# A two-layer decoder trunk: the residual stream held in DRAM by chunks and added to by accumulating transfers, and nine more pairs of weight columns with a second Strassen unit

## The chip, the cores and the metric

The kernel runs on one core of one Trainium2 chip. Its engines are TensorE (PE: matmuls and transposes), VectorE (DVE), ScalarE (ACT), GpSimd (POOL) and SyncE (SP, which only issues transfers); 16 DMA engines move data between DRAM and SBUF, the on-chip memory of 128 partitions. TensorE's sums lie in PSUM. The metric is the device time of one execution in microseconds.

## The reference

The input x is 256 rows of 2048 values, all float32. Each of two layers does

```python
h = rms_norm(x, mix_norm[l])
proj = h @ w_in[l]                                  # 2048 x 7680: q, k, v, uv, gate logits
branch_a = sliding_window_attention(q, k, v, sinks[l]) @ w_attn_branch[l]
branch_b = chunked_sgu(jax.nn.gelu(uv), w_spatial[l], ...) @ w_sgu_branch[l]
gates = jax.nn.sigmoid(gate_logits)
merged = gates[..., :D_MODEL] * branch_a + gates[..., D_MODEL:] * branch_b
x = x + merged @ w_out[l]                           # first residual
h2 = rms_norm(x, ffn_norm[l])
x = x + (jax.nn.silu(h2 @ w_gate[l]) * (h2 @ w_up[l])) @ w_down[l]   # second residual
```

The inner width of the last line (w_gate, w_up, w_down) is 5632. Nearly all the work is products of 256 rows of activations with these weights.

## The kernel before, in words

**Tiles.** The 256 rows are two tiles of 128 (NT = 2). Weights are taken by columns of 512 (a chunk, CW) and by 256 rows of the inner dimension, so that a weight tile is 128 partitions x 1024 values, 512 KB. Activations are kept transposed, in units of 512 inner rows, that is two weight tiles deep.

**Precision.** Each float32 operand is split in two parts that TensorE takes: a high half (ScalarE's copy, `whi` for weights, `uh` for activations) and a low half (VectorE's subtraction, `wlo`, `ul`). A product is three matmuls of 512 columns: high by high, high by low, low by high (L353, L354). One weight tile against both row tiles is 12 matmuls.

**Strassen units.** Columns are often taken in pairs, two chunks against the same activations (gate and up columns of w_gate and w_up; two chunks of w_down, w_out and others). A pair's first unit (number `WINO` = 0) is computed by Strassen's scheme in Winograd's form: the 2 x 2 blocks are the two row tiles, the two inner halves of the unit and the two chunks. Seven products P1 to P7 of 6 matmuls stand for eight. For it VectorE makes four differences of weight tiles (L242, `raw<-raw,raw`), in place; and, once for each unit of activations, four sums (`sums`, L512) from a plain copy of the unit (`flat`), split into `sh` and `sl`. P3, P6 and P7 use these. With `two` a pair does so for unit 1 as well. In the row of gate/up pairs that is done where r > 0 and the pair is one of the round's first three (L190).

**Order.** `plans` lists all pairs and single chunks; `entries` are their weight tiles in TensorE's order, where the P entries of a pair (its head) are woven into the last entries of the plan ahead. `step` works off one entry; `stream.next` keeps the loads 7 entries ahead (`W_LOAD`), the splits 4 (`W_SPLIT`) and the differences 6 (`W_SUM`). `tick` counts slots of two products (some 12 matmuls), and `after(n, fn)` puts work n slots later: turning an activation, its parts, squares for a norm. TensorE runs in the order as written; the other engines' orders are made by a scheduler that models the time, and are fixed in the program. SP issues all weight loads. GpSimd issues the small gathers that finish a transposition (`tt<-box`, 16 transfers of 32 KB behind VectorE's 32 x 32 block transposes), or SP and GpSimd halve them.

**Buffers.** The loaded weight tiles lie in five buffers (`wraw`) plus one buffer for each of the four tiles of a first Strassen unit; those of a second unit take a slot of the pool `big` (26 slots of 4 KB per partition), which also holds activations, boxes, hidden chunks and sums. Split halves have four buffers each (`wsp`). `tmp` has five of 2 KB. The residual stream, `xs`, is one constant tile of 16 KB per partition.

**The stages of a layer**: the input projection (`in`), attention's and the spatial unit's branches (`att`, `sgu`), the output projection (`mix`, two pairs of w_out), then three rounds over the 11 chunks of the inner width, of 4, 4 and 3. A round is so many gate/up pairs (`hidden`), then two w_down pairs over what they made (`hid`). `residual` (L942) adds a product's two row tiles to `xs` straight from PSUM on VectorE (L950); behind the output projection, and behind the last round of layer 0, it also turns the new x for the next norm (`Norm.unit`) and squares it; at the end it stores.

**A unit turned twice.** `again=True` turns a unit of x a second time, on GpSimd's queue, only to make the plain copy and the sums of it for Strassen: for unit 0 of the input projection of layer 0 (L597), and for unit 1 of each layer's gate/up pairs (L963, 24 slots behind the output projection). `summed` (L524) makes them instead from the unit's own halves, `flat = uh + ul`.

**The start.** SP loads x in four chunks with the first weights between; a short transposition gives the norm's columns (`first_cols`), ScalarE scales the transposed x by them (`uh<-pt,first_cols`, L452), and splits the first weights (L257).

## Time and profile before

| | |
|---|---|
| median of 3 runs | 2427.58 us (2427.35 to 2428.07) |
| the profiled execution | 2427.18 us |
| its span, first to last instruction | 2425.5 us |
| bytes read from and written to HBM | 475.27 MB, 2.10 MB |
| instructions | 31042 |

Times in the profile are microseconds, unless ns is written. PE, PEld (loading the stationary operand, beside the matmuls), DVE, ACT and POOL stand with busy time, share and number of instructions. In the groups of instructions a row has line, engine, operation, out<-in with shapes, count, busy time and mean ns of one, then the engine's idle time ahead of them and what ended it; "(+1 forms)" means that another shape is counted in. Line numbers are those of the kernel before, which the change moves down by 4 to 28. In rows by time the first two numbers are start and duration, and a bracket holds idle time and its releaser. In windows each engine has its busy time with the number of instructions, then PEclk, the clock granted to TensorE (1.00 is full), the mean busy share of the DMA engines, and GB/s.

### The profile page before, as it was taken

The numbers are of one execution on the slowest core, as the hardware profiler recorded it, in microseconds if no ns is written. First come the engines' busy times: TensorE is split into PE (matmuls) and PEld (weight loads), VectorE is DVE, ScalarE is ACT, GpSimd is POOL, SyncE is SP. The second block draws the span as 40 slices with busy tenths as digits, with TensorE's granted clock in tenths as the row PEclk, the third lists the DMA queues.
The fourth block names the chain that finished last, engine by engine and source line by source line (L and its number), as shares of the span: only waits on it lengthen the run. The fifth ranks groups of instructions, "written<-read, shape, count | busy, mean of one in ns | idle before, by whom it ended". The sixth has DMA issues, their size and how long they took to land.

```text
span 2425.5 us, 31042 instructions
## 1 busy us (share of the span) xinstructions
PE 2417.2 (100%) x10768; PEld 1984.1 (82%) x10768; DVE 2025.9 (84%) x2346; ACT 1492.1 (62%) x1878; POOL 290.7 (12%) x545
## 2 busy tenths in 40 slices
PE   9999999999999999999999999999999999999999
PEld 7877888888888888888888778888888888888887
DVE  6789787897978997899887897878878789978996
ACT  5577555566655675567655775555666556655664
POOL 3100001032110011001101000011322101110010
PEclk9999999999999999999999999999999999999999
DMA  9665678576767657766747557775767676667664
GB/s 294 213 187 162 182 201 251 175 252 208 225 209 235 208 175 227 237 200 178 231 149 261 173 158 195 217 227 181 249 207 235 204 245 185 204 211 236 210 181 146
DMA packets 278989, 504.62 MB, mean 208 GB/s; under 512 B 27760, under 2 KB 39120, under 8 KB 278832
## 3 DMA queue, kind: packets, MB, share of 16 engines
q1 hardware_dynamic: 262288, 485.83, 64.4%
q0 software_dynamic: 16224, 16.54, 2.6%
q8 instruction: 84, 1.38, 0.2%
q14 instruction: 73, 0.60, 0.1%
q10 hardware_dynamic: 320, 0.27, 0.0%
HBM read 475.27 MB, written 2.10 MB: 197 GB/s over the span
## 4 chain that ended last, share of the span: by engine, by line
PE 96%; DMA 2%; DVE 1%; issue 0%; ACT 0%; POOL 0%; SPq 0%; DVEq 0%; ACTq 0%
PE acc L353 63%; PE acc L354 31%; DMA raw<-in_w_in_dram 2%; PE psc L798 1%; PE po L850 0%; DVE wlo L258 0%; PE psg L933 0%; PE ppt L835 0%; ACT whi L257 0%; PE pt L466 0%; POOL rq L325 0%; DVE ul L457 0%; SPq L290 0%; DVE xs L950 0%; DVE box L423 0%
## 5 line engine op out<-in xcount | busy, mean ns | idle before, releaser
L257 ACT ACTIVATE whi<-raw 128x1024 fp32r<-128x1024 f32 (+1 forms) x1086 | 1142.5, 1058 | 843.1 <-PE acc L354 559.9
L258 DVE TENSOR_TENSOR wlo<-raw,whi 128x1024 fp32r<-128x1024 f32 (+1 forms) x1087 | 1314.9, 1219 | 344.5 <-ACT whi L257 329.1
L353 PE MATMUL acc<-whi,uh 128*128 128x512 f32 x2954 | 1154.5, 391 | 0.9 <-ACT uh L452 0.9
L353 PE MATMUL acc<-wlo,uh 128*128 128x512 f32 x2954 | 1150.7, 390 | 2.0 <-DVE wlo L258 2.0
L354 PE MATMUL acc<-whi,ul 128*128 128x512 f32 x2954 | 1150.0, 389 | 0.0
L353 PEld LDWEIGHTS acc<-whi,uh 128*128 128x128 f32 x2954 | 554.5, 188 | 121.3 <-issue 3.8
L353 PEld LDWEIGHTS acc<-wlo,uh 128*128 128x128 f32 x2954 | 554.6, 188 | 119.3 <-DVE wlo L258 4.5
L354 PEld LDWEIGHTS acc<-whi,ul 128*128 128x128 f32 x2954 | 554.6, 188 | 115.8 <-DVE ul L457 0.5
L429 POOL DMA_DIRECT2D tt<-box x496 | 243.0, 497 | 1632.2 <-DVE box L423 747.5
L242 DVE TENSOR_TENSOR raw<-raw,raw 128x1024 f32<-128x1024 f32 x252 | 307.4, 1220 | 1.7 <-DMA raw<-in_w_up_dram 0.8
L353 PE MATMUL acc<-whi,sh 128*128 128x512 f32 x504 | 197.9, 393 | 0.0
L353 PE MATMUL acc<-wlo,sh 128*128 128x512 f32 x504 | 196.5, 390 | 0.0
L354 PE MATMUL acc<-whi,sl 128*128 128x512 f32 x504 | 196.2, 389 | 0.0
L353 PEld LDWEIGHTS acc<-whi,sh 128*128 128x128 f32 x504 | 94.6, 188 | 22.1 <-issue 2.3
L353 PEld LDWEIGHTS acc<-wlo,sh 128*128 128x128 f32 x504 | 94.7, 188 | 19.9 <-DVE wlo L258 0.8
L354 PEld LDWEIGHTS acc<-whi,sl 128*128 128x128 f32 x504 | 94.6, 188 | 19.8
L379 DVE TENSOR_TENSOR kept<-acc,kept 128x512 f32<-128x512 f32 x102 | 69.8, 684 | 10.3 <-PE acc L354 10.3
L382 ACT ACTIVATE acc<-kept 128x512 f32<-128x512 f32 x102 | 59.6, 587 | 5.1 <-DVE kept L379 4.2
L950 DVE SCALAR_TENSOR_TENSOR xs<-acc,xs 128x512 f32<-128x512 f32 (+1 forms) x66 | 42.0, 668 | 8.4 <-PE acc L354 8.0
L325 POOL TENSOR_TENSOR rv<-ve,neg_half 128x4 f32<-128x4 f32 x8 | 10.2, 1272 | 260.7 <-DVE ve L898 241.8
L376 ACT ACTIVATE kept<-acc 128x512 f32<-128x512 f32 x51 | 30.3, 594 | 8.4 <-PE acc L354 7.9
L820 ACT ACTIVATE pr<-pr,negm 128x128 f32<-128x128 f32 x64 | 24.9, 389 | 14.1 <-DVE negm L811 14.1
(145 smaller groups left out, 840.9 us busy)
## 6 DMA issues: line engine op xcount, KB each, us to landing
raw<-in_w_in_dram SPq DMA_DIRECT2D x239, 512.0 KB, 4.8
raw<-in_w_gate_dram SPq DMA_DIRECT2D x176, 512.0 KB, 4.6
raw<-in_w_up_dram SPq DMA_DIRECT2D x176, 512.0 KB, 5.0
raw<-in_w_down_dram SPq DMA_DIRECT2D x176, 512.0 KB, 5.0
raw<-in_w_out_dram SPq DMA_DIRECT2D x64, 512.0 KB, 6.2
raw<-in_w_attn_branch_dram SPq DMA_DIRECT2D x64, 256.0 KB, 6.3
raw<-in_w_sgu_branch_dram SPq DMA_DIRECT2D x32, 512.0 KB, 5.9
tt<-box POOLq DMA_DIRECT2D x496, 32.0 KB, 4.4
```

The lines of the kernel that those rows point to most:

```text
L242: self.last = nc.vector.tensor_tensor(out=self.raws[d], in0=self.raws[x], in1=self.raws[y], op=ALU.subtract)
L257: self.high = nc.scalar.activation(hi[:, i, :], raw[:, i, :], AF.Copy)
L258: self.last = nc.vector.tensor_tensor(out=lo[:, i, :], in0=raw[:, i, :], in1=hi[:, i, :].bitcast(F32), op=ALU.subtract)
L353: nc.tensor.matmul(ps, a, part[:, kk, :], start=first and kk + n == 0, stop=False, skip_group_check=True)
L354: nc.tensor.matmul(ps, b, hi[:, kk, :], start=False, stop=kk == 1, skip_group_check=True)
L376: nc.scalar.activation(p.kept[:, 1, :], a[0], AF.Copy)
L379: nc.vector.tensor_tensor(out=p.kept[:, int(tag == "P7"), :], in0=a[1], in1=p.kept[:, 1, :], op=ALU.add)
L382: nc.scalar.activation(ps, p.kept[:, t, :], AF.Copy)
L429: q.dma_start(dst[j * B:(j + 1) * B, i], box[i * B:(i + 1) * B, j])
L798: nc.tensor.matmul(pscore[:, i, :nk], self.qT[pair // 4][j * HD:(j + 1) * HD, pair % 4, t * P:(t + 1) * P], self.kT[j * HD:(j + 1) * HD, : ...
L820: self.exps = nc.scalar.activation(pr4[:, h, :], pr4[:, h, :], AF.Exp, bias=nm_[:, h:h + 1], accum_out=den[:, h:h + 1])
L950: nc.vector.scalar_tensor_tensor(out=xs[:, t, sl], in0=sums[t][:, i * w:(i + 1) * w], scalar=scale, in1=xs[:, t, sl], op0=ALU.mult, op1=AL ...
```

## The change

**The residual stream.** `xs` goes. At the start x is loaded into four slots of `big`, one per chunk, which serve the first norm alone. The stream's home is a DRAM buffer of four chunks, `held_x` (512 KB each). Behind the output projection and behind layer 0's last round, the four chunks are fetched into slots (issued by GpSimd, slots 2 to 5 of that residual's first pair; for layer 0's output projection from the input x itself), added to on VectorE as before, and stored to `held_x` five slots later. Behind rounds 0 and 1 the chunks are not fetched: ScalarE copies the two row tiles out of PSUM (`part`), and GpSimd issues one transfer a chunk that adds it to `held_x`. The last residual fetches, adds, and stores the output. In all 16 accumulating transfers, 12 stores and 16 fetches (four of them from x).

**Buffers.** 16 KB of `xs`, one buffer of `tmp` and three small constants make room for 31 slots of `big` instead of 26; `tmp` has 4.

**More second Strassen units.** `FFN_TWO` names the gate/up pairs (round, place) that have two: all of round 1's four, the last of round 0, and the three of round 2, in both layers: (0, 3) and (1, 3) are new, four pairs. `HID_TWO` names five w_down pairs (layer, round, first chunk): both of round 0 in each layer, and the second of round 1 in layer 1. Nine pairs in all.

**Sums from the halves.** The three second turnings (`again`) are replaced by `summed`, and the hidden unit 1 of the rounds with a `HID_TWO` pair gets its sums the same way, 16 slots (or 9) behind the pair that made it.

```diff
 W_SPLIT = 4
-W_TWO = 24
+X_FETCH = 2
+HID_TWO = (1, 2, 2), (0, 0, 0), (1, 0, 0), (0, 0, 2), (1, 0, 2)
+W_HID = 16
+FFN_TWO = (1, 0), (1, 1), (1, 2), (2, 0), (2, 1), (2, 2), (0, 3), (1, 3)
+W_TWO = 20
 W_SUM = 6
...
-    big = ctx.enter_context(tc.tile_pool(name="big", bufs=26))
+    big = ctx.enter_context(tc.tile_pool(name="big", bufs=31))
     wraw = ctx.enter_context(tc.tile_pool(name="wraw", bufs=5))
     wsp = ctx.enter_context(tc.tile_pool(name="wsp", bufs=4))
-    tmp = ctx.enter_context(tc.tile_pool(name="tmp", bufs=5))
+    tmp = ctx.enter_context(tc.tile_pool(name="tmp", bufs=4))
...
         for r, (f0, f1) in enumerate(ROUNDS):
             for f in range(f0, f1):
                 plans.append(pair(("ffn", l), w_gate[l, :, f * CW:(f + 1) * CW], w_up[l, :, f * CW:(f + 1) * CW], f == 0,
-                                  two=r > 0 and f - f0 < 3))
+                                  two=(r, f - f0) in FFN_TWO))
             c_ = cols_of(w_down[l, f0 * CW:f1 * CW, :], NCH)
-            plans += [pair(("hid", l, r), c_[j], c_[j + 1], j == 0) for j in range(0, NCH, 2)]
+            plans += [pair(("hid", l, r), c_[j], c_[j + 1], j == 0, two=(l, r, j) in HID_TWO) for j in range(0, NCH, 2)]
...
-    xs = const.tile([P, NT, D], F32, name="xs")
+    def x_rows(dram, c):
+        return dram[0, :, c * CW:(c + 1) * CW].rearrange("(t p) n -> p t n", p=P)
+
+    kept_x = ctx.enter_context(tc.tile_pool(name="kept_x", bufs=1, space=bass.MemoryType.DRAM))
+    held_x = [kept_x.tile([P, NT, CW], F32, tag=f"x{c}", name=f"held_x{c}") for c in range(NCH)]
+    xs = [slot([P, NT, CW], name="x") for _ in range(NCH)]
     for c in range(NCH):
         for t in range(NT):
-            nc.sync.dma_start(xs[:, t, c * CW:(c + 1) * CW],
-                              x[0, t * P:(t + 1) * P, c * CW:(c + 1) * CW])
+            nc.sync.dma_start(xs[c][:, t, :], x[0, t * P:(t + 1) * P, c * CW:(c + 1) * CW])
         stream.load(LOAD_BY[c])
...
         def __init__(self, cols, soon=False):
             self.cols, self.soon = cols, soon
-            self.units = [None] * NCH
+            self.units, self.x = [None] * NCH, [None] * NCH
         def squares(self, c):
             for t in range(NT):
                 junk = temp(name="junk")
-                nc.scalar.activation(junk, xs[:, t, c * CW:(c + 1) * CW], AF.Square,
+                nc.scalar.activation(junk, self.x[c][:, t, :], AF.Square,
                                      accum_out=self.ss[t][:, c:c + 1])
         def unit(self, c, on_pe=False, again=False, queue=nc.gpsimd, late=0):
-            transposed(self.units, c, xs[:, :, c * CW:(c + 1) * CW], cols=self.cols[:, 4 * c:4 * c + 4],
+            transposed(self.units, c, self.x[c], cols=self.cols[:, 4 * c:4 * c + 4],
                        on_pe=on_pe, again=again, queue=queue, late=late,
                        wino=WINO_FIRST if again else None if c != WINO or on_pe else WINO_IN if self.soon else WINO_NORM)
...
     for c in range(NCH):
         after(3 + c, lambda c=c: squared(c))
     after(7, lambda: norm.finish())
-    after(10, lambda: norm.unit(WINO, again=True))
+    after(10, lambda: summed(norm.units, WINO, (1, 2, 4)))
...
                 nc.vector.scalar_tensor_tensor(out=u, in0=pg[:, i], scalar=vcols[:, bc:bc + 1], in1=u,
                                                op0=ALU.add, op1=ALU.mult)
-    def residual(key, nxt=None, scale=1.0, store=False):
+    def residual(key, nxt=None, scale=1.0, store=False, first=False):
+
+        xt = {}
+
+        def fetched(j):
+            xt[j] = slot([P, NT, CW], name="x")
+            nc.gpsimd.dma_start(xt[j], x_rows(x, j) if first else held_x[j])
         def chunk(j, sums):
+            if j not in xt:
+                part = slot([P, NT, CW], name="part")
+                for t in range(NT):
+                    nc.scalar.activation(part[:, t, :], sums[t], AF.Copy)
+                nc.gpsimd.dma_start(held_x[j], part, accum_op=ALU.add)
+                return
             for t in range(NT):
                 n = 2 if store and j == NCH - 1 else 1
                 w = CW // n
                 for i in range(n):
-                    sl = slice(j * CW + i * w, j * CW + (i + 1) * w)
-                    nc.vector.scalar_tensor_tensor(out=xs[:, t, sl], in0=sums[t][:, i * w:(i + 1) * w], scalar=scale,
-                                                   in1=xs[:, t, sl], op0=ALU.mult, op1=ALU.add)
+                    sl = slice(i * w, (i + 1) * w)
+                    nc.vector.scalar_tensor_tensor(out=xt[j][:, t, sl], in0=sums[t][:, sl], scalar=scale,
+                                                   in1=xt[j][:, t, sl], op0=ALU.mult, op1=ALU.add)
                     if store:
                         eng = nc.sync if i == 0 else nc.scalar
-                        eng.dma_start(out[0, t * P:(t + 1) * P, sl], xs[:, t, sl])
+                        eng.dma_start(out[0, t * P:(t + 1) * P, j * CW + i * w:j * CW + (i + 1) * w], xt[j][:, t, sl])
             if nxt is not None:
+                nxt.x[j] = xt[j]
+                after(5, lambda: nc.gpsimd.dma_start(held_x[j], xt[j]))
                 last = j == NCH - 1 and not nxt.soon
                 after(1 if last else 2, lambda: nxt.unit(j, j > 0 and nxt.soon, queue=None if last or j == WINO and not nxt.soon else nc.gpsimd,
                                                          late=-2 if last else 0))
...
                 if j == NCH - 1:
                     after(4, lambda: nxt.finish())
                     if not nxt.soon:
-                        after(W_TWO, lambda: nxt.unit(WINO + 1, again=True))
+                        after(W_TWO, lambda: summed(nxt.units, WINO + 1, (1, 2, 4)))
         for j in range(0, NCH, 2):
+            if j == 0 and (nxt is not None or store):
+                for i in range(NCH):
+                    after(X_FETCH + i, lambda i=i: fetched(i))
             product_pair(key, lambda sums: chunk(j, sums), lambda sums: chunk(j + 1, sums))
         return nxt
...
             merged(j, product(("sgu", l)))
             tick()
-        norm = residual(("mix", l), nxt, scale=0.5)
+        norm = residual(("mix", l), nxt, scale=0.5, first=l == 0)
...
                                          queue=None if soon else nc.gpsimd, late=-2 if c == 3 else 4 if c == 1 and len(hT) == 4 else 2 if c == 2 else 0))
             product_pair(("ffn", l), on_gate, on_up)
+            if c == WINO + 1 and any((l, r, j) in HID_TWO for j in (0, 2)):
+                after(W_HID if f1 < NF else W_HID - 7, lambda: summed(hT, c, (1, 2, 4)))
```

**What moves at the start.** ScalarE's first rows before, up to its seventh weight (`whi` a high half, `uh` a scaled unit of x, `pt` its transposition, `junk` a square for the norm):

```order
L452 ACTIVATE uh_137<-pt_139,first_cols 128x256 x2
L257 ACTIVATE whi_161<-raw_90 128x512
L452 ACTIVATE uh_137<-pt_150,first_cols 128x256 x2
L257 ACTIVATE whi_167<-raw_93 128x512 x2
L257 ACTIVATE whi_173<-raw_97 128x1024
L452 ACTIVATE uh_217<-pt_219,first_cols 128x256 x2
L452 ACTIVATE uh_217<-pt_230,first_cols 128x256 x2
L257 ACTIVATE whi_243<-raw_99 128x1024
L257 ACTIVATE whi_261<-raw_103 128x1024
```

And of the change:

```order
L261 ACTIVATE whi_170<-raw_99 128x512
L261 ACTIVATE whi_176<-raw_102 128x512 x2
L460 ACTIVATE uh_146<-pt_148,first_cols_138 128x256 x2
L460 ACTIVATE uh_146<-pt_159,first_cols_138 128x256 x2
L261 ACTIVATE whi_182<-raw_106 128x1024
L261 ACTIVATE whi_252<-raw_108 128x1024
L261 ACTIVATE whi_270<-raw_112 128x1024
L570 ACTIVATE junk_310,ss_13_144<-x_93 128x512
```

Both parts of the second weight (`whi_176`) now stand ahead of the first scaled unit (`uh_146`), and the next two weights ahead of the second unit. On SP, the loads behind the last chunk of x, before:

```order
L290 DMA xs<-in_x_dram 128x512 x2
L231 DMA raw_199<-in_w_in_dram 128x2x512
L231 DMA raw_1228<-in_w_in_dram 128x2x512
L231 DMA raw_1230<-in_w_in_dram 128x2x512
L231 DMA raw_1316<-in_w_in_dram 128x2x512
L231 DMA raw_1318<-in_w_in_dram 128x2x512
L231 DMA raw_201<-in_w_in_dram 128x2x512
```

And of the change:

```order
L299 DMA x_96<-in_x_dram 128x512 x2
L235 DMA raw_208<-in_w_in_dram 128x2x512
L235 DMA raw_1214<-in_w_in_dram 128x2x512
L235 DMA raw_210<-in_w_in_dram 128x2x512
L235 DMA raw_1216<-in_w_in_dram 128x2x512
L235 DMA raw_1302<-in_w_in_dram 128x2x512
```

The weight that was the sixth load behind that chunk (`raw_201`) is now the third (`raw_210`); those of the first pair's Strassen unit (`raw_1228` to `raw_1318` before, from `raw_1214` on now) stand behind it but for one.

**What moves in round 1's fourth pair**, on VectorE, layer 0 (`raw<-raw,raw` a difference of weights, `wlo` a split, `ul` and `sl` the low halves of a hidden unit and of its sums; `flat` is the plain hidden unit). Before:

```order
L498 TENSOR_TENSOR ul_7380<-flat_7634,uh_7379 128x1024
L258 TENSOR_TENSOR wlo_7791<-raw_7712,whi_7790 128x1024
L242 TENSOR_TENSOR raw_7712<-raw_7714,raw_7712 128x1024
L512 TENSOR_TENSOR sums_7807<-flat_7634 128x256
L258 TENSOR_TENSOR wlo_7817<-raw_7731,whi_7816 128x1024
L512 TENSOR_TENSOR sums_7807<-sums_7807,flat_7634 128x256
L258 TENSOR_TENSOR wlo_7827<-raw_7712,whi_7826 128x1024
L512 TENSOR_TENSOR sums_7807<-flat_7634 128x256
L512 TENSOR_TENSOR sums_7807<-flat_7634,sums_7807 128x256
L258 TENSOR_TENSOR wlo_7839<-raw_7788,whi_7838 128x1024
L242 TENSOR_TENSOR raw_7712<-raw_7814,raw_7712 128x1024
L258 TENSOR_TENSOR wlo_7854<-raw_7810,whi_7853 128x1024
```

Of the change, the rows from the difference ahead of `ul` on:

```order
L246 TENSOR_TENSOR raw_7689<-raw_7691,raw_7689 128x1024
L506 TENSOR_TENSOR ul_7394<-flat_7658,uh_7393 128x1024
L262 TENSOR_TENSOR wlo_7824<-raw_7410,whi_7823 128x1024
L246 TENSOR_TENSOR raw_7709<-raw_7711,raw_7709 128x1024
L520 TENSOR_TENSOR sums_7836<-flat_7658 128x256
L262 TENSOR_TENSOR wlo_7842<-raw_7689,whi_7841 128x1024
L520 TENSOR_TENSOR sums_7836<-sums_7836,flat_7658 128x256
L262 TENSOR_TENSOR wlo_7852<-raw_7709,whi_7851 128x1024
```

and the eight that follow:

```order
L520 TENSOR_TENSOR sums_7836<-flat_7658 128x256
L520 TENSOR_TENSOR sums_7836<-flat_7658,sums_7836 128x256
L262 TENSOR_TENSOR wlo_7870<-raw_7447,whi_7869 128x1024
L246 TENSOR_TENSOR raw_7689<-raw_7761,raw_7689 128x1024
L262 TENSOR_TENSOR wlo_7885<-raw_7839,whi_7884 128x1024
L246 TENSOR_TENSOR raw_7709<-raw_7798,raw_7709 128x1024
L506 TENSOR_TENSOR sl_7881<-sums_7836,sh_7880 128x1024
L262 TENSOR_TENSOR wlo_7896<-raw_7689,whi_7895 128x1024
```

The pair behind that (w_down) is unchanged; the fourth pair itself now has differences of two units, so that `raw_7689` and `raw_7709` stand in turn, each difference ahead of its split.

**What moves on GpSimd**, from the end of round 0 of layer 0 to the gathers of round 1. Before:

```order
L429 DMA tt_5253<-box_5254 32x256 x16
L429 DMA tt_5386<-box_5387 32x256 x16
L429 DMA tt_5609<-box_5610 32x256 x16
L429 DMA tt_6007<-box_6008 32x256 x16
L429 DMA tt_6316<-box_6317 32x256 x8
L429 DMA tt_7381<-box_7382 32x256 x16
L429 DMA tt_7728<-box_7729 32x256 x16
```

Of the change:

```order
L437 DMA tt_5592<-box_5593 32x256 x16
L437 DMA tt_6037<-box_6038 32x256 x16
L437 DMA tt_6378<-box_6379 32x256 x8
L964 DMA held_x_89<-part_6655 128x1024
L964 DMA held_x_90<-part_6725 128x1024
L964 DMA held_x_91<-part_6902 128x1024
L964 DMA held_x_92<-part_7052 128x1024
L437 DMA tt_7395<-box_7396 32x256 x16
L437 DMA tt_7746<-box_7747 32x256 x16
```

Four accumulating transfers (`held_x<-part`) now stand between one round's gathers and the next's; the gathers for unit 1 of the gate/up pairs (`tt_5386` before) are gone.

7 lines of the change are left out of this document (4 added, 3 removed).

## The prediction

> **What bounds the kernel now.** I read the page's first part, then the chain of waits, then busy time by stretch, then the order of time at the tightest place.
>
> ```profile
> span 2425.5 us, 31042 instructions
> PE 2417.2 (100%) x10768; PEld 1984.1 (82%) x10768; DVE 2025.9 (84%) x2346; ACT 1492.1 (62%) x1878; POOL 290.7 (12%) x545
> PE 96%; DMA 2%; DVE 1%; issue 0%; ACT 0%; POOL 0%; SPq 0%; DVEq 0%; ACTq 0%
> ```
>
> TensorE is idle for 8.3 us of the span, and the chain lies on it. So a matmul less is worth its pitch, as long as VectorE, next at 84%, still delivers. Here are five stretches: a plain gate/up pair (661.1), a plain w_down pair (703.3) and the pair behind it, then two pairs that already have two Strassen units:
>
> ```profile
> core 0: us, PE busy (x) PEld busy (x) DVE busy (x) ACT busy (x) POOL busy (x), PEclk, DMA share, GB/s
> 661.10:703.30 42.20, 42.20 (x188) 34.94 (x187) 32.33 (x32) 25.43 (x29) 7.83 (x16) 1.00 0.70 211
> 703.30:745.40 42.10, 42.10 (x187) 34.88 (x186) 33.33 (x34) 22.19 (x23) 3.91 (x8) 1.00 0.80 249
> 745.40:794.40 49.00, 49.00 (x218) 40.55 (x217) 41.31 (x40) 28.42 (x30) 0.00 (x0) 1.00 0.71 229
> 794.40:835.20 40.80, 40.80 (x182) 33.78 (x181) 37.12 (x35) 25.13 (x26) 0.00 (x0) 1.00 0.56 177
> 835.20:876.00 40.80, 40.80 (x181) 33.78 (x180) 38.15 (x36) 28.00 (x34) 7.84 (x16) 1.00 0.63 192
> ```
>
> The clock is 1.00, and TensorE never rests. A pair with one unit has 186 matmuls (42.2 us), one with two has 180 (40.8 us); the counts in the rows hold one or two of a neighbour. So the pitch is 40.8/180 = 0.227 us. In 835 to 876 VectorE is at 38.15 of 40.8, and its place in time shows what is left:
>
> ```profile
> 860.54 0.68 DVE L379 TENSOR_TENSOR kept<-acc,kept 128x512 f32<-128x512 f32 x1
> 861.14 1.22 DVE L258 TENSOR_TENSOR wlo<-raw,whi 128x1024 fp32r<-128x1024 f32 x1
> 862.28 1.22 DVE L242 TENSOR_TENSOR raw<-raw,raw 128x1024 f32<-128x1024 f32 x1
> 862.39 0.39 PE L353 MATMUL acc<-whi,uh 128*128 128x512 f32 x1
> 862.62 0.39 PE L353 MATMUL acc<-wlo,uh 128*128 128x512 f32 x1
> ```
>
> The low half of a weight is done at 862.36 and read at 862.62: a margin of 0.26 us and no wait. Back to back, such an operation costs 1.14 us (861.14 to 862.28), since 0.08 us of its 1.22 overlap the next.
>
> **The matmuls.** A unit multiplied plainly takes four entries of 12 matmuls, a Strassen unit seven of 6: 42 for 48. Nine pairs lose 6 each, and TensorE's order has 54 rows fewer. 54 x 0.227 = **12.2 us off**. This term is sure; that the change doesn't do what it says is excluded.
>
> **What VectorE pays.** Groups of its operations:
>
> ```profile
> L258 DVE TENSOR_TENSOR wlo<-raw,whi 128x1024 fp32r<-128x1024 f32 (+1 forms) x1087 | 1314.9, 1219 | 344.5 <-ACT whi L257 329.1 <-DMA tt<-box 3.0 <-DMA raw<-in_w_out_dram 3.0
> L242 DVE TENSOR_TENSOR raw<-raw,raw 128x1024 f32<-128x1024 f32 x252 | 307.4, 1220 | 1.7 <-DMA raw<-in_w_up_dram 0.8
> L950 DVE SCALAR_TENSOR_TENSOR xs<-acc,xs 128x512 f32<-128x512 f32 (+1 forms) x66 | 42.0, 668 | 8.4 <-PE acc L354 8.0
> L512 DVE TENSOR_TENSOR sums<-flat 128x256 f32<-128x256 f32 x32 | 13.3, 420 | 0.5 <-ACT flat L493 0.5
> L382 ACT ACTIVATE acc<-kept 128x512 f32<-128x512 f32 x102 | 59.6, 587 | 5.1 <-DVE kept L379 4.2 <-DVE gate L1011 0.6
> ```
>
> Each of the nine adds three splits and four subtractions: 7 x 1.14 = 8.0 us of VectorE in a pair that gets 1.4 us shorter. Three w_down rounds need sums of a second unit of activations (flat, four sums, low half: 2 x 1.14 + 4 x 0.34 = 3.6 us, the four being rows of 420 ns less the overlap). Against that, 32 residual adds (0.6 us each with overlap, 19 us in all) go to ScalarE as copies of about 0.59 us; it is at 62% and hides them. Replacing the second transposition of one unit (three places) by sums takes 48 small gathers off GpSimd and leaves VectorE's bill nearly as it was.
>
> Where does this exceed TensorE? I added these prices along VectorE's order, from split to split, against 12 or 6 matmuls of 0.227 us for each; a split can be done at most four weight tiles ahead (four buffers). On the old order this sum gives 0.8 us as the smallest margin in the stretch 835 to 876, where the trace has 0.26, so it is some 0.5 us too kind. In the new order all old places keep a margin; five places lose theirs:
>
> - Both layers, pair 3 of round 0 and the w_down pair behind it: 42.7 + 39.1 us of VectorE beside 40.9 + 40.9 of TensorE. 0.2 us late.
> - Both layers, pair 3 of round 1: in the rows shown with the change, 12 operations of 1.14 and four sums of 0.34 are 15.0 us beside 10.9 us of matmuls, with 3.1 us ahead: 1.0 us late, and 0.1 behind it.
> - The end of layer 1: 37.8 beside 38.1, with splits and subtractions bunched at its close: 0.9 us late.
>
> That is 2 x (0.2 + 1.1) + 0.9 = 3.5 us; with 0.5 more at each of five places, 6.0. I take **4.5 us on**, since a wait of TensorE at the first place gives VectorE time for the next. The bounds are 0 (ScalarE and buffers as kind as the sum at its best) and 12 (a pair at 42.7 that also waits for its high halves in each of its parts).
>
> **The start.**
>
> ```profile
> 6.78 0.84 ACT L452 ACTIVATE uh<-pt,first_cols 128x256 fp32r<-128x256 f32 x2 [4.03 <-DVE first_cols L308]
> 7.31 0.50 PE L353 MATMUL acc<-whi,uh 128*128 128x512 f32 x1 [0.93 <-ACT uh L452]
> 8.75 1.16 ACT L257 ACTIVATE whi<-raw 128x512 fp32r<-128x512 f32 x2
> 15.34 1.06 ACT L257 ACTIVATE whi<-raw 128x1024 fp32r<-128x1024 f32 x1 [0.66 <-DMA raw<-in_w_in_dram]
> 27.71 1.23 DVE L258 TENSOR_TENSOR wlo<-raw,whi 128x1024 fp32r<-128x1024 f32 x1 [5.18 <-ACT whi L257]
> 27.73 0.50 PE L353 MATMUL acc<-whi,uh 128*128 128x512 f32 x1
> 29.00 0.51 PE L353 MATMUL acc<-wlo,uh 128*128 128x512 f32 x1 [0.76 <-DVE wlo L258]
> ```
>
> In the new order ScalarE splits the second weight (done at 9.9) before it scales the first unit of x, so the first product starts some 2.9 us later, and the second unit stands behind the fifth weight (here at 16.4). What comes back: the wait for the weight split at 27.71, where two matmuls start 1.27 us apart instead of 0.227, so 1.0 us and some 0.3 behind it; SP now issues that weight three loads earlier. Net 2.9 - 1.3 = **1.6 us on**, between 0 (loads were the limit all along) and 2.9 (nothing comes back).
>
> **The transfers.** 16 accumulating, 12 storing and 16 fetching ones of 512 KB, all issued by GpSimd:
>
> ```profile
> q1 hardware_dynamic: 262288, 485.83, 64.4%
> L318 POOL DMA_DIRECT2D cs<-in_cosine_dram x1 | 0.9, 882 | 0.0
> raw<-in_w_out_dram SPq DMA_DIRECT2D x64, 512.0 KB, 6.2
> 7.30:34.80 27.50, 25.93 (x120) 20.32 (x121) 19.93 (x61) 20.98 (x43) 5.42 (x10) 1.00 0.98 346
> 449.40:492.50 43.10, 43.10 (x196) 35.76 (x195) 36.75 (x39) 24.30 (x29) 3.91 (x8) 1.00 0.70 228
> ```
>
> By the nearest rows: 0.88 us of GpSimd each (39 us on an engine at 12%), and, at 485.83 MB for 64.4% of the span, 1.7 us of all 16 engines. An accumulating one I bound by one and three such passes (read, read, write): 1.7 to 5.1 us. They lie beside matmuls in stretches where the engines are at 56 to 80%. The four fetches ahead of an output projection (the stretch from 449.4) come over some 11 us, at 2.1 MB / 11 us = 190 GB/s beside 228. Together that is more than the 346 of the start, where the engines are full, and may put weights back by 2 to 3 us; a weight buffer is freed some 12 us (52 matmuls) before its next use and w_out lands in 6.2, so that is covered. **The added wait**: an accumulating transfer waits on GpSimd for its two copies on ScalarE and for the same chunk's last transfer, more than a hundred us back; behind it stand the next chunk's transfer and, some 40 us later, the next round's gathers. The gathers that a unit waits for in the same pair stand behind a store or a fetch at most. I take 0. With the cover gone each of the 44 holds weights back by a quarter of its 1.7 us or more (the engines' idle share is a quarter): 44 x 0.4 = 18 us. Nothing says that it gains.
>
> **Sum**, against the profiled execution's own 2427.18 us (span 2425.5, 1.7 around it): 2427.2 - 12.2 + 4.5 + 1.6 = 2421.1. The median shown stands 0.4 above that execution, so **2421.5 us**.
>
> **Rivals.** Changes under 0.2% (4.9 us, that is from 2422.7 to 2432.4) count as none.
>
> *VectorE absorbs it*: ScalarE lends it what the sum took away, and the start's delay vanishes behind loads. For it: at 0.26 us of margin TensorE still didn't wait. 2427.6 - 12.2 + 1 = 2416.4.
>
> *VectorE becomes the bound*: a late split delays the buffer, that the high half, that the next split, and the lateness is met in all of the row of seven two-unit pairs instead of at one place. For it: the row's VectorE work, by the sum, is 104% of TensorE's in two of the pairs and 96% in one. Against it: the other four are at 86 to 93%, and the sum met the old margin within 0.6 us. With 12 us of waits, 2427.6 - 12.2 + 12 + 1.6 = 2429.0: no change.
>
> *Slower: the transfers put weights back.* Place: the w_down pairs of round 0, where the next pair's first Strassen weights are loaded into single buffers freed 6.8 us (five entries of 1.36) before their use, just when a chunk is accumulated. Price: a landing of 5 us that shares the engines with a pass of 5.1 takes up to 10, 3 us over. It decides from a landing of about 7 us on; if each of the accumulating and storing transfers costs 0.7 us, 28 x 0.7 = 20 us, so 2427.6 - 12.2 + 20 = 2435. Against it: mean load there is 211 to 249 GB/s, and a first product has over 2 us of margin in the sum.
>
> *Slower: GpSimd's issuing holds VectorE up.* If each issue stops a subtraction for its 0.88 us, the 12 per layer between the output projection and the end of round 1 (four stores, eight accumulating) cost 24 x 0.88 = 21 us, most of it bare: 2436. Against it:
>
> ```profile
> 399.00:420.80 21.80, 21.80 (x98) 18.06 (x97) 13.53 (x16) 11.22 (x14) 11.38 (x24) 1.00 0.90 260
> L258 DVE TENSOR_TENSOR wlo<-raw,whi 128x1024 fp32r<-128x1024 f32 x9 | 11.0, 1218 | 8.3 <-ACT whi L257 6.8 <-DMA tt<-box 1.5
> ```
>
> GpSimd issues for 11.38 of these 21.8 us, and the subtraction takes 1218 ns, as everywhere. [...]
>
> **Chances.** Forecast 0.50 (2418 to 2425: 0.38 of it faster, 0.12 no change); absorbed 0.19; VectorE the bound 0.19 (no change); transfers slower 0.09; ports 0.03. So faster 0.57, no change 0.31, slower 0.12. The range runs from below the absorbing case (2416.4) to above the bound one (2429.0) and leaves out the two slower ones and a little beside: 2415 to 2430.
>
> **What would show it.** Right: 54 matmuls fewer at 0.227 us; waits of TensorE on wlo of 2 to 6 us near the fourth pairs of rounds 0 and 1 and in the last two w_down pairs; a first product near 10 us; raw landings near 5 us. Wrong: waits for wlo spread over all two-unit pairs, high halves that wait for raw transfers in w_down pairs, subtractions longer than 1.22 us, or GpSimd issues of many us. A start as early as before, or margins as wide as the old ones, would make it faster than forecast.

## The result, and the profile after

The changed kernel takes 2431.86 us, the median of 21 runs (2430.04 to 2434.18), against 2427.58 for the kernel before (21 runs, 2426.20 to 2430.24). The ratio is 1.0017, 95% interval 1.0011 to 1.0023: slower by 4.3 us. That lies inside the 0.2% called no change (the interval's upper end, 0.23%, lies a little outside), but on the other side of zero than forecast and above the range of 2415 to 2430. The profiled execution took 2430.28 us, 3.1 more than that of before.

The first part of the page and the shares of the chain:

```profile
span 2428.5 us, 31047 instructions
PE 2412.2 (99%) x10714; PEld 1974.3 (81%) x10714; DVE 2080.1 (86%) x2392; ACT 1526.9 (63%) x1928; POOL 294.9 (12%) x541
PE 86%; DVE 6%; DMA 4%; issue 2%; ACT 1%; SPq 1%; POOL 0%; DVEq 0%; ACTq 0%; POOLq 0%
```

The 54 matmuls are gone (10768 to 10714), VectorE has 54.2 us more, and the chain, which was TensorE's for 96%, is now for 14% elsewhere: it leaves TensorE where TensorE waits, for 6% to VectorE and for 4% (2% before) to transfers. Busy time by stretch: the fourth gate/up pair of round 0, the two w_down pairs behind it, the third pair of round 1, the next to last w_down pair of layer 1, each with the head of the pair behind it woven into its end (the columns as in the prediction):

```profile
670.10:713.30 43.20, 41.96 (x182) 33.57 (x181) 41.59 (x45) 28.58 (x33) 7.84 (x16) 1.00 0.71 224
713.30:755.10 41.80, 41.09 (x181) 33.70 (x180) 40.62 (x39) 26.96 (x30) 4.83 (x9) 1.00 0.68 201
755.10:796.70 41.60, 41.14 (x181) 33.71 (x180) 35.40 (x33) 27.27 (x32) 1.73 (x2) 1.00 0.85 262
878.30:920.20 41.90, 41.37 (x181) 33.63 (x180) 41.63 (x44) 27.75 (x30) 7.84 (x16) 1.00 0.60 187
2366.90:2408.10 41.20, 39.84 (x176) 32.23 (x177) 38.31 (x38) 26.40 (x30) 0.00 (x0) 1.00 0.51 169
```

180 matmuls of 0.227 us are 40.9, so the first stretch lost 2.3 us, the second 0.9, the third 0.7, the fourth 1.0. (The last one holds 168 matmuls and the counts some of a neighbour: 41.2 - 38.1 = 3.1, of which 0.9 was there before.) In the first and the fourth VectorE is busy for 41.6 us, more than TensorE needs. In the second it is at 40.6 and in the third at 35.4, which is less. Taken over all pairs in this way, against the same pair of the kernel before:

| place | predicted | layer 0 | layer 1 |
|---|---|---|---|
| round 0, fourth gate/up pair and the two w_down pairs | 0.2 | 2.4 + 1.8 | 2.4 + 0.6 |
| round 1, head of the fourth pair and what follows | 1.1 | 1.5 | 1.5 |
| end of layer 1 | 0.9 | - | 2.8 |
| start, net | 1.6 | 2.2 | - |

The waits are 13.0 us (the expectations below go by a first count of 12.6); with the start's 2.2 and 12.2 off this is +3.0, which is what the two spans differ by (2428.5 and 2425.5). Everywhere else the two kernels run alike to 0.1 us, with two moves of half a us in layer 1's first stage that cancel.

What TensorE waited for, over the whole span (us in total, times, longest; four rows of seven):

```profile
PE acc L361 <- DVE wlo L262: 4.6, 7, 1.4
PE acc L361 <- ACT uh L460: 3.7, 1, 3.7
PE acc L361 <- ACT acc L385: 1.1, 2, 0.7
PE acc L361 <- ACT whi L261: 0.7, 2, 0.4
```

Late splits lead, as forecast; the second row is the start. What made the splits late is not the same everywhere. At round 0's and round 1's fourth pairs (2 x 2.4 + 2 x 1.5 = 7.8 us) VectorE comes out of a long run of work with hardly a gap. Ahead of the largest waits in the w_down pairs (5.2 us in all), an engine stands still for a weight that has not landed. Three rows, from the first and the second w_down pair behind round 0 of layer 0, and from the end of layer 1:

```profile
729.37 1.23 DVE L246 TENSOR_TENSOR raw<-raw,raw 128x1024 f32<-128x1024 f32 x1 [0.70 <-DMA raw<-in_w_down_dram]
772.58 1.22 DVE L246 TENSOR_TENSOR raw<-raw,raw 128x1024 f32<-128x1024 f32 x1 [1.31 <-DMA raw<-in_w_up_dram]
2369.01 2.01 ACT L261 ACTIVATE whi<-raw 128x1024 fp32r<-128x1024 f32 x2 [5.39 <-DMA raw<-in_w_down_dram]
```

The chain passes through landings of 6.4, 6.7 and 8.0 us there, and from each by differences, high halves, splits or a copy on ScalarE to a matmul that waits (at 735, 774 and 2379 us). In the kernel before neither VectorE nor ScalarE waits for a weight between 660 and 800 us. The sums of TensorE's waits are smaller than the time lost: a matmul is drawn 0.39 long and they start 0.227 apart, so a wait costs 0.2 us or so more than its row says, and the first matmul behind it is drawn longer (0.50 us; the next starts 0.34 behind it).

### The profile page after: what moved, and what is told of

It reads as the page before. It is cut to its first block, busy times and chain, and to the rows that moved or that the text cites. A ratio compares the mean times of both kernels' runs of the same rounds, so it can differ in the third digit from the quotient of the medians.

```text
span 2428.5 us, 31047 instructions
## 1 busy us (share of the span) xinstructions
PE 2412.2 (99%) x10714; PEld 1974.3 (81%) x10714; DVE 2080.1 (86%) x2392; ACT 1526.9 (63%) x1928; POOL 294.9 (12%) x541
## 4 chain that ended last, share of the span: by engine, by line
PE 86%; DVE 6%; DMA 4%; issue 2%; ACT 1%; SPq 1%; POOL 0%; DVEq 0%; ACTq 0%; POOLq 0%
PE acc L361 56%; PE acc L362 28%; DVE wlo L262 3%; DMA raw<-in_w_up_dram 2%; DVE raw L246 1%; DMA raw<-in_w_down_dram 1%; DMA tt<-box 1%; ACT whi L261 1%; PE psc L807 1%; PE po L859 0%; SPq L437 0%; PE pt L474 0%; POOL tt L437 0%; PE psg L942 0%; PE ppt L844 0%
## 5 line engine op out<-in xcount | busy, mean ns | idle before, releaser
L261 ACT ACTIVATE whi<-raw 128x1024 fp32r<-128x1024 f32 (+1 forms) x1113 | 1163.2, 1057 | 807.0 <-PE acc L362 467.1
L262 DVE TENSOR_TENSOR wlo<-raw,whi 128x1024 fp32r<-128x1024 f32 (+1 forms) x1114 | 1339.6, 1216 | 290.4 <-ACT whi L261 277.0
L361 PE MATMUL acc<-whi,uh 128*128 128x512 f32 x2864 | 1120.4, 391 | 3.7 <-ACT uh L460 3.7
L361 PE MATMUL acc<-wlo,uh 128*128 128x512 f32 x2864 | 1117.5, 390 | 1.6 <-DVE wlo L262 0.9
L362 PE MATMUL acc<-whi,ul 128*128 128x512 f32 x2864 | 1115.9, 390 | 0.0
L437 POOL DMA_DIRECT2D tt<-box x448 | 220.1, 499 | 1188.0 <-DVE box L431 436.3
L246 DVE TENSOR_TENSOR raw<-raw,raw 128x1024 f32<-128x1024 f32 x288 | 350.6, 1218 | 5.2 <-DMA raw<-in_w_up_dram 2.9
L361 PE MATMUL acc<-wlo,sh 128*128 128x512 f32 x576 | 225.6, 392 | 3.9 <-DVE wlo L262 3.7
L361 PE MATMUL acc<-whi,sh 128*128 128x512 f32 x576 | 226.3, 393 | 1.8 <-ACT acc L385 1.1
L362 PE MATMUL acc<-whi,sl 128*128 128x512 f32 x576 | 224.4, 390 | 0.0
```

The lines of the kernel that those rows point to most:

```text
L246: self.last = nc.vector.tensor_tensor(out=self.raws[d], in0=self.raws[x], in1=self.raws[y], op=ALU.subtract)
L261: self.high = nc.scalar.activation(hi[:, i, :], raw[:, i, :], AF.Copy)
L262: self.last = nc.vector.tensor_tensor(out=lo[:, i, :], in0=raw[:, i, :], in1=hi[:, i, :].bitcast(F32), op=ALU.subtract)
L361: nc.tensor.matmul(ps, a, part[:, kk, :], start=first and kk + n == 0, stop=False, skip_group_check=True)
L362: nc.tensor.matmul(ps, b, hi[:, kk, :], start=False, stop=kk == 1, skip_group_check=True)
L437: q.dma_start(dst[j * B:(j + 1) * B, i], box[i * B:(i + 1) * B, j])
```

## The experiments

Differences from "before" are between medians of the same session, where the kernel before ran on the same chip. The diffs are excerpts, without their indentation and with constants written out.

### Which part costs: the stream alone, each kind of pair alone

**e1, the stream without the pairs**, and **e3, e4, one kind of pair each**:

```diff
-HID_TWO = (1, 2, 2), (0, 0, 0), (1, 0, 0), (0, 0, 2), (1, 0, 2)
+HID_TWO = ()                                                          # e1, e3
-FFN_TWO = (1, 0), (1, 1), (1, 2), (2, 0), (2, 1), (2, 2), (0, 3), (1, 3)
+FFN_TWO = (1, 0), (1, 1), (1, 2), (2, 0), (2, 1), (2, 2)              # e1, e4
```

> The residual stream in DRAM, the sums from the halves, the larger pool, but none of the nine second units (so 54 matmuls more than the change). Theory 'late splits' (the change's waits come only from the nine pairs' work on VectorE and ScalarE; the transfers cost nothing): the time before plus the start's 2.2 us and nothing else, 2427.6 + 2.2 = 2429.8, and no wait of TensorE above 0.3 us between 450 and 1200 us that the kernel before lacks. Theory 'transfers' (the 44 transfers of 512 KB put weights back): most of the 12.6 us of waits stay, 2427.6 + 2.2 + 8 or more = 2438 or more.

> The change without the five w_down pairs' second units; the four gate/up pairs keep theirs. 30 matmuls come back (6.8 us). 'Late splits': the waits in the w_down pairs (2.4 us in round 0, 2.8 at the end) go, and those of round 0's fourth pair (2 x 2.4), whose tail is woven with the w_down pair's head, go too, while round 1's 2 x 1.5 stay: 2431.9 + 6.8 - 10 = 2428.7. 'Transfers': waits stay where the accumulating transfers lie, 2431.9 + 6.8 - 3 = 2436.

> The change without the four gate/up pairs' second units (round 0 and round 1, fourth pair); the five w_down pairs keep theirs. 24 matmuls come back (5.4 us). 'Late splits': round 1's waits (2 x 1.5) go, round 0's fourth pair's (2 x 2.4) at least in part, the w_down pairs' stay: 2431.9 + 5.4 - 5 to 8 = 2429.3 to 2432.3. 'Transfers': nothing but the matmuls moves, 2437.

Measured: e1 2428.57, 1.5 above before (ratio 1.0007, 0.9998 to 1.0016); e3 2427.50, 0.4 above (1.0000, 0.9991 to 1.0009); e4 2426.56, 0.6 below (0.9996, 0.9987 to 1.0005). The change itself stood 4.3 above. In e1 no stretch behind the start lost more than 0.15 us: without the pairs the 44 transfers cost TensorE nothing, and the theory "transfers", by which most of the waits would stay in e1, falls. Not that they are small:

```profile
raw<-in_w_out_dram SPq DMA_DIRECT2D x64, 512.0 KB, 7.5
held_x<-part POOLq DMA_DIRECT2D x16, 512.0 KB, 8.6
held_x<-x POOLq DMA_DIRECT2D x12, 512.0 KB, 5.0
x<-held_x POOLq DMA_DIRECT2D x12, 512.0 KB, 8.0
```

These are rows of the change: KB each and median us from issue to landing. An accumulating transfer lands after 8.6 us, a fetch after 8.0, and w_out's weights land in 7.5 instead of 6.2. In e1 such landings are under cover: between 755 and 775 us w_up's weight lands after 7.8 us there (6.3 in the kernel before), and VectorE does not wait for it.

e3 and e4 show that the kinds do not add up. In e3 the fourth pair of round 0, with a plain w_down pair behind it, loses nothing:

```profile
669.80:703.80 34.00, 34.00 (x151) 27.96 (x149) 28.71 (x29) 22.42 (x26) 7.82 (x16) 1.00 0.64 194
```

This is e3's stretch of that pair (150 matmuls, since the next head is short): VectorE is at 28.7 of 34.0. In e4 the w_down pair behind a plain pair loses nothing either; the second loses 0.6, where VectorE waits 1.1 us for a weight of w_up. Only where both kinds stand in a row are 2.4 + 1.8 us lost in layer 0, and VectorE's work exceeds the time in the first of these pairs. Round 1's 1.5 us a layer came in e3 as in the change, and 2.6 of the end's 2.8 in e4, with ScalarE waiting 5.2 us for a weight of w_down. In e1 and e3, which have the end's four fetches but not its new pair, ScalarE does not wait there.

### Is it VectorE's work?

**e5, shorter differences**: in the second units, 128 of 1024 columns are subtracted; the rest of those differences is left out.

```diff
+w = slice(0, 64) if entries[self.summed]["unit"] == WINO + 1 else slice(0, CW)
-self.last = nc.vector.tensor_tensor(out=self.raws[d], in0=self.raws[x], in1=self.raws[y], op=ALU.subtract)
+self.last = nc.vector.tensor_tensor(out=self.raws[d][:, :, w], in0=self.raws[x][:, :, w],
+                                    in1=self.raws[y][:, :, w], op=ALU.subtract)
```

> The change, where the four weight differences of every second Strassen unit are taken over 128 of 1024 columns only (the rest of those differences is left out), so that VectorE has some 4 x 1 us less in each pair with two units, and everything else stays. Theory 'VectorE's work': the waits in the nine new pairs go (9 to 10 of the 12.6 us), 2431.9 - 10 = 2422. Theory 'turns and landings' (the waits come from high halves that stand on ScalarE behind rows waiting for TensorE, and from weights that land late): most stay, 2428 to 2431.

Measured: 2420.05, 7.4 below before (0.9970, 0.9959 to 0.9982), so 11.7 less than the change. The same first stretch of e5:

```profile
669.80:710.60 40.80, 40.80 (x182) 33.68 (x181) 38.00 (x44) 28.73 (x33) 7.83 (x16) 1.00 0.73 235
```

With VectorE at 38.0 of 40.8 us the pair loses nothing, with all splits and transfers of the change still there. So the waits come with VectorE's work. (A shorter difference also lets its high half begin earlier; e5 does not tell the work from that.) What stayed in e5's profiled execution is 3.8 us in layer 1 at that place, and 0.6 in a w_down pair. Both are late weights. The first:

```profile
1888.71 1.23 DVE L247 TENSOR_TENSOR raw<-raw,raw 128x1024 f32<-128x1024 f32 x1 [2.76 <-DMA raw<-in_w_down_dram]
```

The split behind this difference ends at 1891.1, where TensorE has stood for 1.9 us; its granted clock is then 0.61 from 1891.0 to 1895.2, and matmuls start 0.43 us apart. In the w_down pair VectorE stood 1.1 us for a weight of w_up. At the end of layer 1 ScalarE still waited 4.1 us for a weight of w_down, and TensorE lost nothing by it: with less work VectorE made up for a late weight in some places, not in all.

### Or ScalarE's turn?

VectorE and ScalarE of the change ahead of its first large wait, in order of time (start, duration, in brackets the idle time ahead and what ended it):

```profile
683.17 1.22 DVE L552 TENSOR_TENSOR sl<-sums,sh 128x1024 fp32r<-128x1024 f32 x1
684.31 4.62 DVE L262 TENSOR_TENSOR wlo<-raw,whi 128x1024 fp32r<-128x1024 f32 x4
688.85 2.35 DVE L246 TENSOR_TENSOR raw<-raw,raw 128x1024 f32<-128x1024 f32 x2
692.81 3.49 DVE L262 TENSOR_TENSOR wlo<-raw,whi 128x1024 fp32r<-128x1024 f32 x3 [1.61 <-ACT whi L261]
691.15 0.69 ACT L1076 ACTIVATE hid<-acc,rstd 128x512 f32<-128x512 f32 x1 [1.51 <-PE acc L362]
691.73 2.94 ACT L261 ACTIVATE whi<-raw 128x1024 fp32r<-128x1024 f32 x3
694.09 0.50 PE L361 MATMUL acc<-wlo,sh 128*128 128x512 f32 x1 [0.76 <-DVE wlo L262]
```

VectorE works without a gap up to 691.2 and then stands for 1.6 us, because the next high half follows a Silu (`hid<-acc`) on ScalarE that waited for TensorE. I took this for the missing part of my sum.

**e13, the Silu behind the high halves**:

```diff
-for t in range(NT):
-    nc.scalar.activation(hid[:, t, :], g[t], AF.Silu, scale=norm.r[t])
+def act():
+    with tc.issue_after(stream.high.ins):
+        for t in range(NT):
+            nc.scalar.activation(hid[:, t, :], g[t], AF.Silu, scale=norm.r[t])
+after(1, act)
```

> The change, with the two Silu rows of each gate/up pair put one slot later and behind the high halves that are due by then (in round 0's fourth pair three high halves of weights now go ahead of them). Theory 'ScalarE's turn' (in the change VectorE stood idle 1.6 us at 691 us because the next high half stood behind a Silu that waited for TensorE): the wait of 1.1 us at 692 and its like in layer 1 go, 2 to 4 us less than the change, 2428 to 2430. Theory 'VectorE's work alone' (it was busy without a gap for 30 us ahead of that place): waits move a few us on, within 1 us of the change.

Measured: 2433.41, 6.0 above before (1.0025, 1.0014 to 1.0035); the interval overlaps the change's, and no gain is in it. The same place in e13:

```profile
689.60 2.35 DVE L246 TENSOR_TENSOR raw<-raw,raw 128x1024 f32<-128x1024 f32 x2
693.08 3.50 DVE L262 TENSOR_TENSOR wlo<-raw,whi 128x1024 fp32r<-128x1024 f32 x3 [1.12 <-ACT whi L261]
691.99 2.96 ACT L261 ACTIVATE whi<-raw 128x1024 fp32r<-128x1024 f32 x3 [1.59 <-DVE raw L246]
694.36 0.50 PE L361 MATMUL acc<-wlo,sh 128*128 128x512 f32 x1 [0.76 <-DVE wlo L262]
```

The three high halves now go first, and the first of them waits for VectorE's own difference, which ended at 691.95. TensorE waits as long as before. So at this place ScalarE's turn is not what is late; the differences are, at the end of a run of VectorE's work without a gap. And there is a price that the sum did not have: difference (VectorE), high half (ScalarE, 1.06 us), low half (VectorE) is a round trip, and where nothing else is due VectorE stands for its middle, 1.1 us here.

**e6, five buffers for the split halves** (splits five ahead, 29 slots in `big`) and **e10, 29 slots alone**:

```diff
-W_SPLIT = 4
+W_SPLIT = 5                                                    # e6
-    big = ctx.enter_context(tc.tile_pool(name="big", bufs=31))
+    big = ctx.enter_context(tc.tile_pool(name="big", bufs=29))    # e6, e10
-    wsp = ctx.enter_context(tc.tile_pool(name="wsp", bufs=4))
+    wsp = ctx.enter_context(tc.tile_pool(name="wsp", bufs=5))     # e6
```

> The change with five buffers for each split half instead of four, splits five weight tiles ahead, and 29 slots in the big pool instead of 31 to make room. 'VectorE's work' with too little lead (each wait is a bunch of work of 2 to 3 us that more lead would even out): waits fall to a half or less, 2425 or so. If the pairs are simply over 100% of TensorE's time, or the two slots less hold loads back: 2431 or more.

> The change with 29 slots in the big pool instead of 31, and four buffers for split halves as in the change. If the two slots were what cost the run with five buffers its 133 us: 2500 or more, with differences of second units waiting for late loads. If it was its order (splits five ahead stand next to the differences, so that ScalarE and VectorE take turns): within 3 us of the change.

Measured: e6 2564.52, 137 above before (1.0563, 1.0549 to 1.0578); e10 2437.81, 10.4 above (1.0046, 1.0034 to 1.0059). Two slots less cost 6 us, so the pool's last two slots at least are needed; most of e6's loss comes from the rest of its edit. VectorE's largest wait in e6, and in the change:

```profile
DVE wlo L262 <- ACT whi L261: 416.6, 377, 5.2
```

```profile
DVE wlo L262 <- ACT whi L261: 277.0, 318, 5.4
```

VectorE waits 140 us more for ScalarE. With splits five ahead and differences six, a difference stands one tile ahead of its split, which would put ScalarE's middle of the round trip bare; no run shows that this is the reason. More lead alone was not tried with differences moved ahead as well, so whether it would help stays open.

### The start

**e2, ScalarE's old order at the start**:

```diff
-stream.split(W_FIRST)
+stream.split(1)
+with tc.issue_after(scaled_by[0].ins):      # the last scaling of the first unit of x
+    stream.split(W_FIRST)
```

> The change, with ScalarE's first rows put back in the old order (first scaled unit of x ahead of the second weight's split). If the start's loss is ScalarE's order: first product near 7.3 us instead of 10.0, and 2.2 us less than the change, 2431.9 - 2.2 = 2429.7. If loads are the limit there: unchanged, 2431.9.

Measured: 2431.62, 4.5 above before (1.0018, 1.0009 to 1.0027): nothing gained, though the first product came at 8.3 instead of 10.0. In the profiled execution e2 was 2.4 us ahead of the change at the 13th product and 0.6 behind it at 101 us; it waited three times for splits in between, 1.9 us. A part of the start's loss shows in the column PEclk. Windows of 2 us, of the kernel before:

```profile
8.00:10.00 2.00, 1.35 (x5) 0.81 (x5) 2.00 (x8) 1.91 (x5) 0.00 (x0) 1.00 1.04 372
10.00:12.00 2.00, 2.00 (x13) 1.69 (x12) 1.62 (x4) 0.78 (x1) 0.00 (x0) 1.00 1.05 401
```

and of the change:

```profile
8.00:10.00 2.00, 0.00 (x0) 0.00 (x0) 1.34 (x3) 1.55 (x4) 0.00 (x0) 0.70 1.04 395
10.00:12.00 2.00, 1.99 (x5) 1.55 (x6) 2.00 (x8) 1.89 (x4) 0.00 (x0) 0.50 1.05 387
12.00:14.00 2.00, 2.00 (x6) 1.54 (x5) 2.00 (x4) 1.27 (x2) 0.09 (x1) 0.50 1.06 391
```

TensorE stands still for 3.7 us ahead of its first product, and its granted clock falls to 0.50 from about 9 to 15.5 us: 5 or 6 matmuls in 2 us instead of 12 or 13.

**e9, seven idle-work matmuls in that gap**; **e12**, the same with four new pairs; **e11**, three of them with the set order of e8:

```diff
 norm.unit(0, True)
+for i in range(7):                          # 3 in e11
+    nc.tensor.matmul(pw_, warm, warm, start=True, stop=True)
```

> The change with seven more idle-work matmuls (128 x 128, 0.47 us each, result unused) between the first transposition and the first product, where TensorE stood still for 3.7 us in the change and its granted clock then showed 0.50 from 9 to 15 us. Theory 'clock': the first product stays near 10.0 us, the granted clock stays 1.00, the 5.5 us at half rate cost no longer 2.7, so some 2 us less than the change: 2429.7 (by the before of the same session plus 2.2). Theory 'ScalarE's order and loads' (the first product is late, the clock only coincides): unchanged, before plus 4.3.

> Four new pairs and the change's own start, with seven idle-work matmuls ahead of the first product. 'Clock': 2 us less than the same without them (2425.1): 2423. 'Order and loads': 2425.

> Four new pairs, the set order at the start, and three idle-work matmuls ahead of the first product (TensorE stood still for 1.7 us there and the clock fell to 0.50 from 9 to 15 us). 'Clock': 2 us less than the same without them (2423.2): 2421, 6 us under before. 'Order and loads': 2423.

Measured: e9 2430.16, 2.7 above before (1.0009, 1.0000 to 1.0018), 1.6 better than the change, though the two intervals overlap; e12 2424.44, 3.0 below (0.9986, 0.9977 to 0.9994); e11 2423.76, 3.7 below (0.9985, 0.9976 to 0.9994), not better than e8 without them (4.3 below), against its expectation. In the profiled executions e11, at a clock of 1.00, was 2.4 us ahead of e8, at 0.50, by the 13th product (0.5 of it at the first), which is what was expected of the clock; but 1.8 of this was gone by 1340 us, in layer 1's first stage, where the two kernels do the same work. Why is open. With matmuls in the gap the clock does not always stay up: e9's profiled execution still shows 0.50 from 12 to 14 us, e11's shows 1.00 from 6 to 18 us. The mean clock over the span, listed with each run, tells the runs of one kernel apart. (In the profiled executions of the kernel before and of the change no stretch of 20 us behind the first is below 1.00; in those of e9, e11 and e12 the clock shown from 6 to 18 us agrees with the listed means of 0.999, 1.000 and 0.999. So in them the mean tells of the start.)

| kernel | runs at 1.000: median | runs at 0.999 or less: median |
|---|---|---|
| before (sessions of e1 to e15) | 65: 2427.1 | 35: 2428.0 |
| the change | none | 21: 2431.9 |
| e9 | 6: 2429.0 | 5: 2430.9 |
| e12 | 4: 2422.8 | 7: 2424.6 |
| e11 | 9: 2423.6 | 2: 2425.9 |

Within a kernel the lower clock goes with 1 to 2.3 us. The change never had a mean of 1.000 in 21 runs, the kernel before in 65 of 100. By these figures the start's loss is the late product and the clock that falls in the gap. What makes it fall, and from what length of gap on, no run settles: in the profiled executions it stood at 0.50 behind gaps of 3.7 us (the change), 1.7 (e8) and 1.6 (e2) ahead of the first product, and at 1.00 behind 0.9 us (the kernel before).

### Versions that keep what pays

**e7**: four new pairs only, both w_down pairs of round 0 in both layers. **e8**: the same, with the start in a set order (ScalarE scales x before the next splits, SP issues the first 60 entries' loads in the order of use).

```diff
-HID_TWO = (1, 2, 2), (0, 0, 0), (1, 0, 0), (0, 0, 2), (1, 0, 2)
+HID_TWO = (0, 0, 0), (1, 0, 0), (0, 0, 2), (1, 0, 2)
-FFN_TWO = (1, 0), (1, 1), (1, 2), (2, 0), (2, 1), (2, 2), (0, 3), (1, 3)
+FFN_TWO = (1, 0), (1, 1), (1, 2), (2, 0), (2, 1), (2, 2)
-self.loaded = nc.sync.dma_start(dst, src)                                            # this and the next: e8
+with tc.issue_after(self.loaded.ins) if self.asked < 60 else ExitStack():
+    self.loaded = nc.sync.dma_start(dst, src)
-self.high = nc.scalar.activation(hi[:, i, :], raw[:, i, :], AF.Copy)
+n = len(self.parts)
+with tc.issue_after(scaled_by[-1 if n else 1].ins) if n < 9 else ExitStack():
+    self.high = nc.scalar.activation(hi[:, i, :], raw[:, i, :], AF.Copy)
```

> The stream in DRAM with four new pairs only, both w_down pairs of round 0 in each layer (no gate/up pair more than before, not the last w_down pair). From the runs so far: the kernel without the new gate/up pairs, 0.5 us under before, plus 6 matmuls (1.4) less the last pair's waits (2.6): 2425.3, 1.8 us under before. If waits only move: 2427.

> The same, with the start in a set order: ScalarE scales x before it splits the next weights, and SP issues the first 60 weight tiles' loads in the order of their use (the first Strassen unit's four come when due, not among the first). If the start's loss is these orders: first product near 7.5 us, the first 96 matmuls in 24 to 26 us instead of 27.3, and 2 to 4 us less than the run before it: 2421.5 to 2423.3. If loads limit it anyhow: no gain.

Measured: e7 2425.09, 2.4 below before (0.9991, 0.9982 to 1.0000), as added up from the parts; e8 2423.22, 4.3 below (0.9982, 0.9973 to 0.9991). Its first 96 matmuls took 28.7 us in the profiled execution, not the 24 to 26 expected; the clock fell to 0.50 there too. Late weights cost these kernels as well: in e7's second w_down pair of layer 0 VectorE waited 2.7 us for a weight of w_up that took 7.7 to land, and TensorE lost 2.1.

**e14** adds the late Silu of e13 to e11, and **e15** the fourth gate/up pair of round 0, (0, 3) in `FFN_TWO`, to e14.

> Four new pairs, the set order at the start with three idle-work matmuls, and the Silu rows behind the high halves. Against the same without the last edit (3.7 us under before): 'ScalarE's turn': w_down pairs of round 0 lose another 1 us, 4.5 us under before. 'VectorE's work alone': 3.7 under.

> The same with the fourth gate/up pair of round 0 as well, in both layers (six new pairs, 12 matmuls less, 2.7 us). In the change that pair and the w_down pair behind it lost 2 x (2.4 + 1.0) us together. 'ScalarE's turn': with the high halves ahead they lose 2 x 1.5, 1 us worse to 1 us better than four pairs. 'VectorE's work alone': 2 x 3.4 - 2.7 = 4 us worse than four pairs.

Measured: e14 2423.10, 4.3 below (0.9985, 0.9976 to 0.9993), no different from e8 and e11; e15 2438.66, 11.3 above (1.0048, 1.0036 to 1.0061). In e15 the fourth pair of round 0 and the w_down pairs behind it lost 4.5 and 4.7 us, no less than in the change; but it also lost 11 us where no pair was changed, in layer 1's spatial unit and output projection (TensorE waits there for a copy on ScalarE, up to 4.3 us). The run says nothing more on the pair. e8, e11 and e14 beat both kernels, by 0.15 to 0.18% over the one before.

## Why the prediction was wrong

- **The matmuls.** 54 fewer at 0.227: right, 12.2 us.
- **VectorE's price.** The step that failed is "I take 4.5 us on" (0 to 12): a right term, mis-sized; the waits measured 13.0. The places were named, but for the second w_down pair of round 0 (0.8 us in layer 0). The largest, the fourth pair of round 0 with the w_down pairs behind it, had 0.2 us a layer in the sum and lost 4.2 and 3.0. Round 1's fourth pair, where VectorE worked almost without a gap, lost 1.5 against 1.1: there the sum of VectorE's durations was nearly right. It left out two things that the traces show. The first is the round trip: a difference must pass ScalarE before VectorE can split it. By an estimate from the first stretch, 0.7 of the 2.3 us lost are VectorE's work over TensorE's 40.9, and 1.6 are the time that it stood idle for a high half. How much of that 1.6 another order would save is open; in e13 it was 1.1 and TensorE waited as long. The second is the landing of weights, taken as covered: ahead of the largest waits of the w_down pairs (5.2 us in all) VectorE or ScalarE stood for a weight. The check on the old order, 0.5 us too kind, was made at a place where TensorE did not wait, and scaled to five places; it could not show what happens once the lead is used up.
- **The sign.** "VectorE becomes the bound", 2429.0, came near in size with 12 us of waits; I gave it 0.19. Its mechanism came true only in part. e5, 7.4 us under before with the differences shortened, shows that VectorE's work decided; but the lateness was not met in all of the row of seven pairs with two units, and part of it came by late weights. That its number is so near is partly luck.
- **The start.** Net 1.6 on, measured 2.2, with the first product at 10.0 as forecast. That product stood 2.7 us behind the kernel before (2.9 forecast), the 13th 4.1 behind: a further 1.4 us, at a granted clock of 0.50, which the prediction did not consider. Behind that 1.9 us came back, more than the 1.3 forecast.
- **The transfers.** Taken as 0, and 0 in e1, which has them with the change's sums, buffers and start, but without the pairs. GpSimd's issuing slowed no subtraction (1218 ns a difference of weights, 1220 before), so that rival, "ports" among the chances, falls. The rival "the transfers put weights back" falls as a cost of 20 us, and of the transfers alone. But its place was right: in the w_down pairs of round 0, weights for the next pair landed 6.7 us (the change) and 7.7 (e7) behind their issue, and VectorE waited. One of the signs of being wrong, "high halves that wait for raw transfers in w_down pairs", is there as well: 5.4 us at the end of layer 1. The sentence "so that is covered" held for as long as VectorE had margin. Whether the 44 transfers make these weights late, or only the loads of the new pairs and their order on SP, is not shown: no run has the pairs without the transfers.
- **That waits stay near their places** held: behind each heavy run TensorE ran at its pitch again (behind round 0 of layer 0, 361 matmuls from 796.7 to 878.3 us, 0.226 each).

## What to carry to other kernels

Where a cheaper product is paid for on another engine, compare the two engines' work over each run of neighbouring pairs, not pair by pair and not over the whole kernel: VectorE was at 86% of the span, and new pairs paid where they stood apart (e7, with four of them, stands 2.4 us under the kernel before, e1 without them 1.5 above) and cost where both kinds stood in a row. In such a sum a chain that goes to a second engine and back counts with its round trip (here 1.06 us on ScalarE, for which VectorE stood idle 1.1 us in e13), not only with the first engine's share. A landing that cost nothing here by itself (7.8 us for a weight of w_up in e1) was waited for once another edit had spent the margin that covered it (7.7 us in e7, where VectorE waited 2.7). Look at the granted clock in the first windows after any edit that delays the first matmul: in the change, with the first product 2.7 us later, it stood at 0.50.
